# First mixer's heads: a PSUM bank of its own for each of four heads under way, and the grouped heads begun behind a turn's second and third chunk

## The chip, the cores and the metric

The kernel runs on one core of a Trainium2 chip. The metric is the device time of one execution in microseconds (us). Five engines work side by side, each with a queue of its own that it works off in order: PE (TensorE, matrix products into PSUM), DVE (VectorE), ACT (ScalarE), POOL (GpSimd), and SP (SyncE), which here issues the transfers. PSUM has eight banks of 512 fp32 columns by 128 partitions.

## The reference

One inference step of a backbone with two layers, for 128 context tokens and 128 latent tokens, 2048 wide. Layer 0 has the mixer that the change touches: eight heads of latent attention (MLA) and eight of grouped-query attention (GQA) side by side, with one output projection.

```python
def mixer_ab(h, rope, ctx, w_in, g_q, w_q_up, g_kv, w_kv_up, g_qn, g_kn, w_out):
    proj = h @ w_in
    ...
    qb = rmsnorm(proj[..., i2:i3].reshape(b, t, GQA_HEADS, HEAD_DIM), g_qn)
    ...
    qa = (rmsnorm(q_lat, g_q) @ w_q_up).reshape(b, t, MLA_HEADS, MLA_NOPE_DIM + MLA_ROPE_DIM)
    ...
    kv = (ckv_all @ w_kv_up).reshape(b, s, MLA_HEADS, MLA_NOPE_DIM + MLA_V_DIM)
    ...
    out_a = softmax_attention(jnp.concatenate([qa_nope, qa_rope], axis=-1), ka, va, MLA_SCALE)
    out_b = softmax_attention(qb, kb_all, vb_all, HEAD_SCALE)
    out = jnp.concatenate([out_a.reshape(b, t, -1), out_b.reshape(b, t, -1)], axis=-1) @ w_out
    return out, new_ctx
```

`softmax_attention` is a softmax over all keys: a context query sees the 128 context keys, a latent query 128 cached and 128 latent keys. Every sub-layer is modulated by `mod = silu(cond) @ w_ada + b_ada` (shift, scale, gate), and that product is large: the kernel works it off in pieces beside the rest.

## The kernel before

Both groups of tokens go through together as 256 columns, the context first. A weight block comes as fp32 (`raw`), and ACT and DVE split it into `wh` (L248) and `wl` (L249); a product is three matmuls, wh by the high half of the activations, wh by the low half, wl by the high half. `gemm` (L356) does 128 output rows of such a product into one PSUM bank; a call of it is a chunk.

The **heads** of the first mixer are the second half of `mixer_ab`. A loop with h = 0, 2, 4, 6 does two MLA heads and two GQA heads a turn. It calls `gemm` for three chunks of the query weights (WQ: the two heads' `qn`, then their rotated parts `qr`) and for two chunks of the key weights (WK: `kn` of each head, 384 columns); then `values` multiplies out both heads' values for the three blocks of keys (`vm`), and `mla_pair` both heads' scores. ACT copies each chunk out of its bank. The GQA queries lie ready in `qb`; `gqa_query` norms and rotates the next one, `gqa` does one head's scores.

`head_ab` (L895) is a head from its scores on, a generator that goes on by a stage whenever `pump` is called: DVE takes the maxima (L867, L868, `nmx` L872), ACT the exponentials with their sums (L874), DVE scales with the reciprocal sums (`rec` L902, `p` L903, L904), PE transposes three blocks into the one misc bank, ACT copies them out (`pT` L883), PE multiplies with the values into an att bank, and ACT and DVE split that (L248, L249) into `o`, the tile that the trace names `hx`. `o` holds heads 0 to 7 from MLA, 8 to 15 from GQA.

PSUM: three banks go round for the gemms and the value blocks (`acc`), three for scores and head results (`att`), one is `misc`, one `ada`.

Beside the heads two more works run, one step at a `pump`. One is the next modulation's rows on PE (`ada` from `araw`, 32 x 512 each, 16 instructions of the trace to a group). The other, **deep**, does a part of `w_ada` on DVE: `sums` (L525) multiplies a tile of 128 x 1024, `kvb` and `block` in turn, 512 KB each by a transfer on SP, with the conditioning `condb`, and sums it; a tile takes two such instructions, which is called a pair here. The product itself isn't used, and is written to `deep.junk`, `o[:, 6:8]`, where the results of the last two MLA heads come later. Half-way a second `condb` is loaded (L513), and ACT does its Silu (L516, with a load of its function table). Of the 21 pairs that end before the first mixer's output starts anew, 15 use the first half and six the second.

After the heads `out_ab` multiplies by `w_out_ab`. `first_three` does the first three output columns at once, in an order (`PAIR_LATE`) that takes k = 8 to 15 first (GQA), then 0 to 5, and last 6 and 7.

The order of the instructions on each engine isn't written out: the code gives the dependences, and a scheduler at compile time with a cost model of its own orders each queue. Some instructions are pinned to the order of the code (`keep_order`).

Of the kernel before, what the change touches and what calls it, by code (L numbers as in the profile page):

```python
# [16 lines left out]
PSUM = bass.MemoryType.PSUM  # L17

P = 128
# [75 lines left out]
def step_kernel(ctx: ExitStack, tc: tile.TileContext, A: dict):  # L95
# [29 lines left out]
    small = ctx.enter_context(tc.tile_pool(name="small", bufs=4))  # L125
    pacc = ctx.enter_context(tc.tile_pool(name="pacc", bufs=3, space=PSUM))
    pmisc = ctx.enter_context(tc.tile_pool(name="pmisc", bufs=1, space=PSUM))
# [97 lines left out]
    def bank():  # L225
        return T_(pmisc, [P, 512], "misc")

    def att_bank():
        return T_(ppool["att"], [P, 512], "att", bufs=3)

# [101 lines left out]

    def first_three(W, xh, xl, order, mid=None, fixed=False, first=0):


        pin = keep_order if fixed else lambda i: i
        raws = [W.load()[0] for _ in range(3)]
        ps = [T_(pacc, [P, 512], "acc") for _ in range(3)]
        blocks = {(c, h): W.halves(raws[c], 8 * h) for c, h in ((0, first), (1, first), (2, first), (0, 1 - first))}
        count = [0] * 3  # L340
        for n, (c, k) in enumerate(order):
            if mid and n == len(order) // 2:
                mid()
# [12 lines left out]
    def gemm(blocks, xh, xl, n=NT, first=0, between=None, more=None, wider=None):  # L356

        fixed = lambda i: keep_order(i) if between is not None else i  # L360
        ps = T_(pacc, [P, 512], "acc")
        last = len(blocks) - 1
        for i in range(last + 1):
            k = (i + first) % (last + 1)
            wh, wl = blocks[k]
            x0 = more(k) if more and i == 0 else wider(k, 0, n + push.pop(0)) if push else xh(k)
            fixed(pe.matmul(ps[:, :x0.shape[-1]], wh, x0, start=(i == 0), stop=False,
                            skip_group_check=i > 0 and x0.shape[-1] > n))
            if callable(between):
# [463 lines left out]
    def final_rstd(st):  # L833
        cols = [bank(), T_(pacc, [P, 512], "acc")]
# [52 lines left out]

    def scores(q, k):

        s = T_(ppool["att"], [P, 512], "att", bufs=3)  # L890
        for g, ks in KEYS:
            pe.matmul(s[:, ks], q[:, g * T:(g + 1) * T], k[:, ks], start=True, stop=True)
        return s

    def head_ab(pl, s, rs, v, hx, c):  # L895
# [12 lines left out]
        yield  # L908
        o = T_(ppool["att"], [P, 512], "att", bufs=3)
        pe.matmul(o[:, 0:T], v(0), pT[:, 0:T], start=True, stop=True)  # L910
# [5 lines left out]
    def mixer_ab(hx, beside):  # L916
        l = 0
        with tc.tile_pool(name="ab", bufs=1) as ab:
            with tc.tile_pool(name="abp", bufs=1) as pj:
# [187 lines left out]
                def values(c):  # L1107
                    pt = T_(ppool["att"], [P, 512], "att", bufs=3)
                    for g in range(2):
# [106 lines left out]
            with tc.tile_pool(name="abh", bufs=1) as hp:  # L1216
# [24 lines left out]
                def gqa(h):  # L1241
                    k = kg[:, h // 4]
                    return head_ab(hp, scores(qb[:, h], k), rsb[:, h], lambda b: vg[:, b, h // 4], o, 8 + h)

                def values():
# [3 lines left out]
                    for b in range(3):  # L1249
                        ps = T_(pacc, [P, 512], "acc")  # L1250
                        t = slice(b * T, (b + 1) * T)
# [10 lines left out]
                def mla_pair(h, qr, kn, vm):  # L1262
                    s = [T_(ppool["att"], [P, 512], "att", bufs=3) for i in range(2)]
                    for g, ks in KEYS:
# [9 lines left out]
                    for i in range(2):  # L1274
                        start(head_ab(hp, s[i], rsm, lambda b, i=i: vm[:, b, i], o, h + i))

                flush()
                weigh_lambda()
                start(gqa_query(0))
                deep.tiles.append((ab, "kvb"))  # L1280
                deep.junk = o[:, 6:8]
                deep.rate = SIDE["heads"]
                for h in range(0, 8, 2):
                    for i in range(2):
                        ps = gemm(WQ.chunk(), qh, qlo)
                        qn[h + i] = T_(hp, [P, NT], "qn", bufs=4)
                        act.copy(qn[h + i], ps)
                        pump(RATE["heads"])
                    ps = gemm(WQ.chunk(), qh, qlo)
                    ev = T_(tmp, [P, NT], "nt", bufs=4)  # L1290
# [51 lines left out]
    def mixer_c(cp, hx, W, ready, st):  # L1342
# [18 lines left out]
        def turned_product(middle):  # L1361

            ps = [T_(pacc, [P, 512], "acc") for _ in range(2)]
            for k in range(KD):
# [48 lines left out]
        def attend(h, q, k, v):  # L1413
# [3 lines left out]
            for j in range(2):  # L1417
                s = T_(ppool["att"], [P, 512], "att", bufs=3)
                for g, ks in ((0, slice(0, T)), (1, slice(T, 3 * T))):
# [21 lines left out]
            yield  # L1441
            o = T_(ppool["att"], [P, 512], "att", bufs=3)
            pe.matmul(o[:, 0:NT], pT[:, 0:T], v[:, 0], start=True, stop=True)
# [18 lines left out]
            yield  # L1462
            pt = T_(ppool["att"], [P, 512], "att", bufs=3)
            for i in range(2):
# [126 lines left out]
    with banks("pab") as ppool["ada"]:  # L1591
        ppool["att"] = ppool["ada"]
        idle = T_(tmp, [P, 512], "am", bufs=1)
        keep_order(dve.memset(idle, 0.0))
        ps = T_(pacc, [P, 512], "acc")
        for _ in range(WARM):
# [183 lines left out]
```

## Time and profile before

| | us |
|---|---|
| runs | 2303.16, 2305.42, 2304.32 |
| median | 2304.32 |
| profiled execution | 2305.63 |
| its span | 2303.9 |
| heads' first weights to the end of the first three output columns, in the span | 208 to 356 |

The profiled execution has a mean granted clock of 0.995. The page gives busy time by engine, and groups of instructions by line; `acc`, `att`, `misc`, `ada` are PSUM banks, `hx` is `o` there, and `L110` and `L113` are the helpers through which every matmul and transpose goes, so that on PE the tiles tell what an instruction is. A row of the timeline has its start, its duration, engine, line, result and operands, and in brackets the idle time before it with what ended that. A 128-row matmul in fp32 counts twice there.

### The profile page before, as it was taken

To read this page: it belongs to the slowest core of one execution; us is meant where nothing else is said; L and a number is where in the kernel's file an instruction comes from. 1 tells how busy PE (TensorE), PEld (TensorE's weight loads), DVE (VectorE), ACT (ScalarE), POOL (GpSimd) and SP (SyncE) were. 2 spreads that over 40 slices of the span, in tenths; PEclk is the share of its full clock that TensorE was granted. 3 is DMA by queue.
4 is the path that set the end of the run, shared out by engine and by line. 5 is a ranking of instruction groups with operands and counts; after the bars stand their busy time and mean duration, and the time that the engine had idled before them with its cause. 6 is when DMAs were issued, how large, how long until landed. Compare 5 with 4: busy or idle time off the path is not lost.

```text
span 2303.9 us, 47433 instructions
## 1 busy us (share of the span) xinstructions
PE 2271.4 (99%) x19496; PEld 2180.7 (95%) x19496; DVE 1887.7 (82%) x2989; ACT 1197.0 (52%) x1959; POOL 173.5 (8%) x206
## 2 busy tenths in 40 slices
PE   8899999999999999999999999999999999999998
PEld 6788869999999999999999999999999999999998
DVE  4668979989999999999978988898899965666654
ACT  4346555665553355555575454457555434555543
POOL 0001101300000000001130001023000000000011
PEclk9999999999999999999999999999999999999999
DMA  9988878777777777777787888776677755555553
GB/s 380 369 338 302 317 312 342 289 275 264 262 256 290 291 274 259 272 259 257 289 293 292 317 325 313 264 272 227 247 255 262 264 201 188 200 190 195 197 189 127
DMA packets 100121, 617.14 MB, mean 268 GB/s; under 512 B 10752, under 2 KB 18880, under 8 KB 33344
## 3 DMA queue, kind: packets, MB, share of 16 engines
q1 hardware_dynamic: 99904, 614.11, 72.0%
q8 instruction: 153, 2.51, 0.4%
q14 instruction: 64, 0.52, 0.1%
HBM read 609.32 MB, written 4.75 MB: 267 GB/s over the span
## 4 chain that ended last, share of the span: by engine, by line
PE 93%; DVE 3%; DMA 1%; issue 1%; ACT 1%; POOL 1%; SPq 0%; DVEq 0%; ACTq 0%
PE acc L110 87%; PE ada L110 3%; PE att L110 2%; DVE wl L249 1%; DVE hx L525 1%; DMA raw<-w_in_ab 1%; DMA kvb<-w_ada 1%; POOL dev L807 0%; DVE rope L858 0%; PE att L113 0%; PE ada L113 0%; PE misc L110 0%; PE misc L113 0%; ACT wh L248 0%; DVE x L1637 0%
## 5 line engine op out<-in xcount | busy, mean ns | idle before, releaser
L110 PE MATMUL acc<-hx,wh 128*128 128x256 f32 (+1 forms) x7264 | 1254.3, 278 | 4.8 <-ACT wh L248 1.7
L248 ACT CAST wh<-raw 128x1024 fp32r<-128x1024 f32 (+1 forms) x834 | 796.1, 967 | 868.1 <-PE acc L110 741.0
L249 DVE TENSOR_TENSOR wl<-raw,wh 128x1024 fp32r<-128x1024 f32 (+1 forms) x834 | 924.9, 1125 | 247.9 <-ACT wh L248 240.7
L110 PEld LDWEIGHTS acc<-hx,wh 128*128 128x128 f32 x7264 | 1099.5, 188 | 23.4 <-issue 8.1
L110 PE MATMUL acc<-hx,wl 128*128 128x256 f32 (+1 forms) x3632 | 1006.8, 277 | 4.4 <-DVE wl L249 4.3
L110 PEld LDWEIGHTS acc<-hx,wl 128*128 128x128 f32 x3632 | 684.1, 188 | 8.1 <-DVE wl L249 5.6
L110 PE MATMUL acc<-g,wh 128*128 128x256 f32 x2816 | 478.8, 276 | 0.0
L110 PEld LDWEIGHTS acc<-g,wh 128*128 128x128 f32 x2816 | 423.4, 188 | 0.0
L110 PE MATMUL acc<-g,wl 128*128 128x256 f32 x1408 | 388.0, 276 | 0.0
L473 DVE CUSTOM_DVE_ANT_0 junk<-araw,condb 128x2048 f32<-128x2048 f32 x128 | 294.3, 2299 | 0.0
L110 PEld LDWEIGHTS acc<-g,wl 128*128 128x128 f32 x1408 | 264.2, 188 | 0.0
L110 PE MATMUL acc<-hxc,wh 128*128 128x256 f32 (+1 forms) x1056 | 189.1, 281 | 0.0
L211 POOL TENSOR_TENSOR sqacc<-sqacc,sq 128x256 f32<-128x256 f32 x62 | 71.5, 1153 | 1507.7 <-ACT sq L207 1507.5
L110 PEld LDWEIGHTS acc<-hxc,wh 128*128 128x128 f32 x1056 | 161.9, 188 | 1.8 <-issue 1.7
L110 PE MATMUL acc<-hxc,wl 128*128 128x256 f32 (+1 forms) x528 | 146.8, 278 | 0.0
L110 PEld LDWEIGHTS acc<-hxc,wl 128*128 128x128 f32 x528 | 99.5, 188 | 0.2
L110 PE MATMUL acc<-wh,hxc 128*128 128x256 f32 (+1 forms) x512 | 95.0, 283 | 0.8 <-DVE nt L818 0.8
L1530 ACT ACTIVATE cv<-acc,convw 128x256 f32<-128x256 f32 x169 | 94.4, 559 | 0.0
L525 DVE CUSTOM_DVE_ANT_0 hx<-block,condb 128x1024 fp32r<-128x1024 f32 x65 | 79.3, 1219 | 6.2 <-DMA block<-w_ada 6.0
L1536 DVE SCALAR_TENSOR_TENSOR cv<-acc,convw,cv 128x254 f32<-128x254 f32 x169 | 81.0, 479 | 3.2
L843 DVE SCALAR_TENSOR_TENSOR x<-acc,mod,x 128x128 f32<-128x128 f32 x190 | 57.2, 343 | 32.0 <-PE acc L110 32.0
L110 PEld LDWEIGHTS acc<-wh,hxc 128*128 128x128 f32 x512 | 79.4, 188 | 3.7 <-issue 2.5
(265 smaller groups left out, 1784.5 us busy)
## 6 DMA issues: line engine op xcount, KB each, us to landing
raw<-w_up SPq DMA_DIRECT2D x176, 1024.0 KB, 4.8
araw<-w_ada SPq DMA_DIRECT2D x136, 1024.0 KB, 6.0
raw<-w_down SPq DMA_DIRECT2D x88, 1024.0 KB, 4.8
raw<-w_in_c SPq DMA_DIRECT2D x48, 1024.0 KB, 6.4
block<-w_ada SPq DMA_DIRECT2D x41, 512.0 KB, 6.4
raw<-w_in_ab SPq DMA_DIRECT2D x18, 1024.0 KB, 9.2
raw<-w_out_ab SPq DMA_DIRECT2D x16, 1024.0 KB, 7.9
raw<-w_out_c SPq DMA_DIRECT2D x16, 1024.0 KB, 7.1
```

The costliest lines, as they stand in the source:

```text
L110: return self.placed(nc.tensor.matmul(*a, **kw))
L211: eng.tensor_tensor(out=st["acc"], in0=st["acc"], in1=sq, op=ALU.add)
L248: pin(act.copy(out_hi, src))
L249: pin(dve.tensor_tensor(out=out_lo, in0=src, in1=out_hi.bitcast(F32), op=ALU.subtract))
L473: keep_order(dve.tensor_tensor_reduce(out=T_(feat["pool"], [P, D], "junk"), in1=feat["row"][:, c], in0=feat["raw"].rearrange("p g n -> p ( ...
L525: keep_order(dve.tensor_tensor_reduce(out=self.junk, in0=self.raw, in1=self.row[:, c].rearrange("p (g n) -> p g n", g=2), scale=1.0, scala ...
L843: dve.scalar_tensor_tensor(out=x[:, c, s], in0=ps[:, s], scalar=mod[:, l, 3 * which + 2, c, g:g + 1], in1=x[:, c, s], op0=ALU.mult, op1=AL ...
L1530: pin(act.activation(y, ps, AF.Identity, scale=cw[:, 1, m:m + 1], bias=cw[:, 3, m:m + 1]))
L1536: pin(dve.scalar_tensor_tensor(out=y3[:, :, :T - 1], in0=p3[:, :, 1:], scalar=cw[:, 2, m:m + 1], in1=y3[:, :, :T - 1], op0=ALU.mult, op1=A ...
```

## The change

- The three gemm banks get names, acc0 to acc2, one buffer each, and `acc_bank` takes them in turn. During the heads' loop only acc0 and acc1 are in that turn. The three att banks get names in the same way.
- A GQA head's scores go to att0 or att1 by the parity of the head; an MLA pair's to att2 and acc2.
- `head_ab` puts its product with the values in the bank of the scores, in place of a new att bank.
- `begin_gqa` starts the first GQA head of a turn behind the second chunk and the second behind the third; both began ahead of a WK chunk before, behind the third and the fourth.
- `first_three` takes acc0, acc1 and att0.

```diff
@@ -123,7 +123,7 @@
     small = ctx.enter_context(tc.tile_pool(name="small", bufs=4))
-    pacc = ctx.enter_context(tc.tile_pool(name="pacc", bufs=3, space=PSUM))
+    pacc = ctx.enter_context(tc.tile_pool(name="pacc", bufs=1, space=PSUM))
     pmisc = ctx.enter_context(tc.tile_pool(name="pmisc", bufs=1, space=PSUM))
...
@@ -225,8 +225,18 @@
 
-    def att_bank():
-        return T_(ppool["att"], [P, 512], "att", bufs=3)
+    def att_bank(n=None):
+        if n is None:
+            turn["att"], n = (turn["att"] + 1) % 3, turn["att"]
+        return T_(ppool["att"], [P, 512], f"att{n}")
+
+    accs, turn = [0, 1, 2], {"acc": 0, "att": 0}
+
+    def acc_bank(n=None):
+        if n is None:
+            n = accs[turn["acc"] % len(accs)]
+            turn["acc"] += 1
+        return T_(pacc, [P, 512], f"acc{n}")
 
...
@@ -330,12 +340,12 @@
 
-    def first_three(W, xh, xl, order, mid=None, fixed=False, first=0):
+    def first_three(W, xh, xl, order, mid=None, fixed=False, first=0, third=acc_bank):
 
 
         pin = keep_order if fixed else lambda i: i
         raws = [W.load()[0] for _ in range(3)]
-        ps = [T_(pacc, [P, 512], "acc") for _ in range(3)]
+        ps = [acc_bank(), acc_bank(), third()]
         blocks = {(c, h): W.halves(raws[c], 8 * h) for c, h in ((0, first), (1, first), (2, first), (0, 1 - first))}
...
@@ -885,9 +895,8 @@
 
-    def scores(q, k):
-
-        s = T_(ppool["att"], [P, 512], "att", bufs=3)
+    def scores(s, q, k):
+
         for g, ks in KEYS:
...
@@ -906,7 +915,7 @@
         yield
-        o = T_(ppool["att"], [P, 512], "att", bufs=3)
+        o = s
         pe.matmul(o[:, 0:T], v(0), pT[:, 0:T], start=True, stop=True)
...
@@ -1240,14 +1249,14 @@
                     k = kg[:, h // 4]
-                    return head_ab(hp, scores(qb[:, h], k), rsb[:, h], lambda b: vg[:, b, h // 4], o, 8 + h)
+                    return head_ab(hp, scores(att_bank(h % 2), qb[:, h], k), rsb[:, h], lambda b: vg[:, b, h // 4], o, 8 + h)
 
                 def values():
 
                     wh, wl = WK.last_tile()
                     vm = T_(hp, [P, 3, 2, P], "vm", bufs=2)
                     for b in range(3):
-                        ps = T_(pacc, [P, 512], "acc")
+                        ps = acc_bank()
                         t = slice(b * T, (b + 1) * T)
...
@@ -1274,8 +1283,14 @@
 
+                def begin_gqa(h):
+                    if h < 7:
+                        start(gqa_query(h + 1))
+                    start(gqa(h))
+
                 flush()
                 weigh_lambda()
+                accs[:] = [0, 1]
                 start(gqa_query(0))
...
@@ -1286,6 +1301,7 @@
                         pump(RATE["heads"])
+                    begin_gqa(h)
                     ps = gemm(WQ.chunk(), qh, qlo)
...
@@ -1294,16 +1310,15 @@
                     kn = []
+                    begin_gqa(h + 1)
                     for i in range(2):
-                        if h + i < 7:
-                            start(gqa_query(h + i + 1))
-                        start(gqa(h + i))
                         ps = gemm(WK.chunk(), kh, klo, 3 * T)
                         kn.append(T_(hp, [P, 3 * T], "kn", bufs=2))
                         act.copy(kn[i], ps)
                         pump(RATE["heads"])
                     mla_pair(h, qr, kn, values())
                 flush()
+                accs[:] = [0, 1, 2]
 
...
@@ -1317,7 +1332,8 @@
         deep.rate = SIDE["out0"]
-        ready = first_three(W, oh, ol, PAIR_LATE, first=1)
+        turn["acc"] = 0
+        ready = first_three(W, oh, ol, PAIR_LATE, first=1, third=lambda: att_bank(0))
         for c in range(KD):
...
```

The remaining hunks only write `acc_bank()` and `att_bank()` where a bank was asked for by its pool. The number of instructions of every kind is the same. Their order differs in the heads and at the start of the output projection only.

PE, the end of the first turn's values and the MLA scores (`kn` and `qr`). Before, the end of the next turn's third query chunk, behind which the first pair's scores stand:

```order
L110 MATMUL acc_505_2847<-ql_290_1787,wl_498_2810 128x256
L110 MATMUL acc_505_2847<-ql_290_1787,wh_497_2809 128x256 x2
L110 MATMUL acc_505_2847<-ql_290_1787,wl_498_2810 128x256
L110 MATMUL att_474_2720<-pT_471_2700,vg_17_119 128x128 x3
L110 MATMUL ada_476_2729<-araw_446_2591,condw_6_79 32x512 x4
L110 MATMUL ada_476_2729<-araw_448_2595,condw_6_79 32x512 x4
L110 MATMUL att_479_2742<-kn_441_2567,qn_406_2425 128x128
L110 MATMUL att_480_2743<-kn_457_2629,qn_415_2474 128x128
L110 MATMUL att_479_2742<-kr_15_117,qr_425_2512 128x128
L110 MATMUL att_480_2743<-kr_15_117,qr_425_2512 128x128
L110 MATMUL att_479_2742<-kn_441_2567,qn_406_2425 128x256
L110 MATMUL att_480_2743<-kn_457_2629,qn_415_2474 128x256
```

Now, the first turn's first value block (`kv_in`):

```order
L110 MATMUL acc1_469_2673<-wl_450_2583,kv_in_289_1786 128x256
L110 MATMUL acc1_469_2673<-wh_449_2582,kv_in_289_1786 128x256 x2
L110 MATMUL acc1_469_2673<-wl_450_2583,kv_in_289_1786 128x256
L110 MATMUL acc1_469_2673<-wh_449_2582,kv_in_289_1786 128x256
L110 MATMUL att2_477_2740<-kn_452_2599,qn_406_2425 128x128
L110 MATMUL att2_477_2740<-kr_15_117,qr_432_2531 128x128
L110 MATMUL att2_477_2740<-kn_452_2599,qn_406_2425 128x256
L113 MATMUL misc_453_2601<-cst_2_74,p_422_2489 128x128
L110 MATMUL att2_477_2740<-kr_15_117,qr_432_2531 128x256
L113 MATMUL misc_453_2601<-cst_2_74,p_422_2489 128x128 x2
```

The first MLA head's scores moved from behind the next turn's three query chunks, a product with values and an ada group to right behind the first value block of their own turn.

ACT, the first turn's key chunks. `p` with `nmx` is an exponential, `kn` and `vm` are the copies of a gemm's bank. Before:

```order
L1291 COPY nt_424_2510<-acc_423_2491 128x256
L1293 COPY qr_425_2512<-nt_424_2510 128x128
L1303 COPY kn_441_2567<-acc_440_2554 128x384
L1229 ACTIVATE sq_516_2914<-qb_47_242 128x256
L1230 ACTIVATE qb_47_242<-qb_47_242,cst_2_74 128x256
L874 ACTIVATE p_432_2533,sums_431_2532<-att_429_2528,nmx_433_2534,rsb_20_122 128x128
L874 ACTIVATE p_432_2533,sums_431_2532<-att_429_2528,nmx_433_2534,rsb_20_122 128x256
L248 CAST wh_495_2805<-raw_494_2803 128x1024
L1303 COPY kn_457_2629<-acc_456_2616 128x384
L1257 COPY vm_466_2661<-acc_467_2662 128x256
```

Now:

```order
L1307 COPY nt_431_2529<-acc0_430_2510 128x256
L1238 ACTIVATE sq_503_2845<-qb_47_242 128x256
L1309 COPY qr_432_2531<-nt_431_2529 128x128
L1239 ACTIVATE qb_47_242<-qb_47_242,cst_2_74 128x256
L884 ACTIVATE p_422_2489,sums_421_2488<-att0_419_2484,nmx_423_2490,rsb_20_122 128x128
L884 ACTIVATE p_422_2489,sums_421_2488<-att0_419_2484,nmx_423_2490,rsb_20_122 128x256
L1317 COPY kn_452_2599<-acc1_451_2586 128x384
L258 CAST wh_493_2803<-raw_492_2801 128x1024
L1317 COPY kn_463_2648<-acc0_462_2635 128x384
L1266 COPY vm_468_2672<-acc1_469_2673 128x256
```

The copy of the first `kn` stood ahead of the first exponential, and now stands behind it.

DVE, the end of the deep pairs ahead of the last MLA heads' split (`hx` from `att` or `acc`; `ISA` is an instruction of a pair). Before:

```order
L902 RECIPROCAL rec_745_3890<-sums_742_3882 128x2
L249 TENSOR_TENSOR wl_769_4049<-raw_755_3927,wh_768_4048 128x512
L525 ISA hx_394_2383,mod_4_77<-kvb_733_3854,condb_605_3291 128x1024
L525 ISA mod_4_77 128x1
L903 TENSOR_SCALAR p_743_3883<-p_743_3883,rec_745_3890 128x128
L904 TENSOR_SCALAR p_743_3883<-p_743_3883,rec_745_3890 128x256
L249 TENSOR_TENSOR wl_769_4049<-raw_755_3927,wh_768_4048 128x512
L249 TENSOR_TENSOR wl_771_4073<-raw_756_3929,wh_770_4072 128x512 x2
L249 TENSOR_TENSOR wl_782_4166<-raw_780_4163,wh_781_4165 128x1024
L723 TENSOR_TENSOR u_753_3924<-mod_4_77,u_753_3924 128x4x2
L249 TENSOR_TENSOR hx_394_2383<-att_750_3906,hx_394_2383 128x256
L249 TENSOR_TENSOR hx_394_2383<-att_751_3912,hx_394_2383 128x256
```

Now:

```order
L535 ISA hx_394_2383,mod_4_77<-block_710_3766,condb_608_3315 128x1024
L535 ISA mod_4_77 128x1
L535 ISA hx_394_2383,mod_4_77<-block_710_3766,condb_608_3315 128x1024
L535 ISA mod_4_77 128x1
L535 ISA hx_394_2383,mod_4_77<-kvb_719_3840,condb_608_3315 128x1024
L535 ISA mod_4_77 128x1
L535 ISA hx_394_2383,mod_4_77<-kvb_719_3840,condb_608_3315 128x1024
L535 ISA mod_4_77 128x1
L259 TENSOR_TENSOR hx_394_2383<-att2_720_3844,hx_394_2383 128x256
L259 TENSOR_TENSOR hx_394_2383<-acc2_721_3845,hx_394_2383 128x256
```

The two splits stood behind weight splits that followed the last pair, and now stand right behind the last pair, of which there are two in a row that wait for their own transfers.

More of the change, by code (lines that the diff above doesn't have):

```diff
@@ L833, in final_rstd @@
     def final_rstd(st):
-        cols = [bank(), T_(pacc, [P, 512], "acc")]
+        cols = [bank(), acc_bank()]
         for src, start in ((st["acc"], True), (st["last"], False)):
@@ L1107, in values @@
                 def values(c):
-                    pt = T_(ppool["att"], [P, 512], "att", bufs=3)
+                    pt = att_bank()
                     for g in range(2):
@@ L1249, in values @@
                     for b in range(3):
-                        ps = T_(pacc, [P, 512], "acc")
+                        ps = acc_bank()
                         t = slice(b * T, (b + 1) * T)
@@ L1262, in mla_pair @@
                 def mla_pair(h, qr, kn, vm):
-                    s = [T_(ppool["att"], [P, 512], "att", bufs=3) for i in range(2)]
+                    s = [att_bank(2), acc_bank(2)]
                     for g, ks in KEYS:
@@ L1361, in turned_product @@
         def turned_product(middle):
-            ps = [T_(pacc, [P, 512], "acc") for _ in range(2)]
+            ps = [acc_bank() for _ in range(2)]
             for k in range(KD):
@@ L1417, in attend @@
             for j in range(2):
-                s = T_(ppool["att"], [P, 512], "att", bufs=3)
+                s = att_bank()
                 for g, ks in ((0, slice(0, T)), (1, slice(T, 3 * T))):
@@ L1441, in attend @@
             yield
-            o = T_(ppool["att"], [P, 512], "att", bufs=3)
+            o = att_bank()
             pe.matmul(o[:, 0:NT], pT[:, 0:T], v[:, 0], start=True, stop=True)
@@ L1462, in attend @@
             yield
-            pt = T_(ppool["att"], [P, 512], "att", bufs=3)
+            pt = att_bank()
             for i in range(2):
@@ L1594, in step_kernel @@
         keep_order(dve.memset(idle, 0.0))
-        ps = T_(pacc, [P, 512], "acc")
+        ps = acc_bank()
         for _ in range(WARM):
```

## The prediction

> **What bounds the kernel now.** The page first: it says which engine sets the span.
>
> ```profile
> PE 2271.4 (99%) x19496; PEld 2180.7 (95%) x19496; DVE 1887.7 (82%) x2989; ACT 1197.0 (52%) x1959; POOL 173.5 (8%) x206
> ```
>
> PE is busy 99% of the span, so a change that leaves its instructions as they are can gain only what PE waits for, and what the clock loses behind a wait. The second view is therefore PE's waits between 208 and 356 us, from the first chunk of the heads to the end of the first three output columns; outside it the order of the instructions is the same in both kernels. Columns: engine, what waited, what it waited for, us in total, times, longest.
>
> ```profile
> PE misc L113 <- DVE p L903: 2.9, 2, 2.7
> PE acc L110 <- ACT vm L1257: 1.7, 2, 1.4
> PE att L110 <- DVE hx L249: 1.2, 1, 1.2
> PE misc L113 <- ACT pT L883: 0.6, 1, 0.6
> PE att L110 <- ACT pT L883: 0.2, 1, 0.2
> ```
>
> They sum to 6.6 us in 148. The change speaks of the second and third (a bank that is not yet read out); the longest waits for DVE to scale a head's probabilities. The third view, windows around that longest one (length, PE busy, PEld, DVE, ACT, POOL, granted clock, DMA share, GB/s), shows what it costs beyond itself.
>
> ```profile
> 325.00:329.00 4.00, 4.00 (x32) 2.91 (x24) 3.63 (x9) 0.74 (x2) 0.00 (x0) 1.00 0.73 260
> 329.00:332.00 3.00, 0.29 (x2) 0.30 (x3) 2.26 (x10) 1.92 (x7) 0.93 (x2) 0.77 0.98 411
> 332.00:336.00 4.00, 4.00 (x19) 0.77 (x18) 3.01 (x6) 0.76 (x3) 0.00 (x0) 0.50 0.71 245
> 336.00:339.00 3.00, 3.00 (x23) 2.88 (x20) 2.56 (x8) 1.44 (x3) 0.00 (x0) 0.76 0.91 363
> ```
>
> After the wait PE runs at half clock: of the last 0.3 us of the second row, the 4.00 of the third and 1.4 of the fourth (0.76 is about 1.44 us at half in 3), 5.7 us of work, half of which, 2.9 us, is lost. [...] The stage thus holds 6.6 + 2.9 = 9.5 us: the most that the change can bring.
>
> The fourth view is DVE from the heads' first weights to the end of the fifteenth pair of its deep reductions (L525, 1024 columns against a transfer of 512 KB), and what it waits for there.
>
> ```profile
> 210.30:301.40 91.10, 82.34 (x208) 1.00 0.84 322
> ```
>
> ```profile
> DVE hx L525 <- DMA block<-w_ada: 5.4, 4, 2.5
> DVE hx L525 <- DMA kvb<-w_ada: 2.2, 2, 1.3
> ```
>
> DVE is busy 82.3 of 91.1 us, and 7.6 of its 8.8 idle us wait for those transfers. It is the second bound, and it works in order.
>
> **The change part by part.** *Banks.* The count of every kind of instruction stays. The gemms of the stage rotate over two banks in place of three, so a gemm now writes the bank of the chunk two back. The first place where this shows is the first block of values in the first turn. Before, it starts at 223.91, and no bank is late:
>
> ```profile
> 222.46 1.07 PE L110 MATMUL ada<-araw,condw 128*32 128x512 f32 x8
> 223.46 0.44 PE L110 MATMUL acc<-kv_in,wh 128*128 128x384 f32 x1
> 223.91 0.28 PE L110 MATMUL acc<-wh,kv_in 128*128 128x256 f32 x1
> ```
>
> On ACT, and on DVE the maxima that release it, the same moments were these:
>
> ```profile
> 223.18 0.46 ACT L874 ACTIVATE p<-att,nmx,rsb 128x128 f32<-128x128 f32 x1 [1.73 <-DVE nmx L872]
> 223.63 0.56 ACT L874 ACTIVATE p<-att,nmx,rsb 128x256 f32<-128x256 f32 x1
> 224.17 1.04 ACT L248 CAST wh<-raw 128x1024 fp32r<-128x1024 f32 x1
> 225.11 0.48 ACT L1303 COPY kn<-acc 128x384 f32<-128x384 f32 x1
> ```
>
> ```profile
> 222.99 0.15 DVE L872 SCALAR_TENSOR_TENSOR nmx<-mx,rsb 128x2 f32<-128x2 f32 x1
> ```
>
> In the new order one half of an ada group (223.46 - 222.46 = 1.00 us) no longer stands ahead, so PE arrives at 222.9. The block now needs the bank whose read-out (kn) stands on ACT behind the first grouped head's two exponentials (223.18 to 224.17, the read of the sum included). Their maxima come some 1 us earlier than 222.99, since the scores do: 222.15 + 1.0 + 0.48 = 223.6. That is a new PE wait of 0.7 us, bounded by 0 (maxima 1 us earlier still) and 2 (as late as before: 224.17 + 0.48 - 222.9 = 1.75). Behind it on PE stand the block itself and the MLA scores, which need its bank order; later turns have more distance between chunk and copy, so I put all four turns at W = 1.5 us, with 0 and 8 as ends.
>
> *Heads' own banks, and where they begin.* The MLA scores no longer wait for an att bank that another head's result holds (the 1.2 us row), and stand a turn's third earlier. More of PE's work thereby stands ahead of the first output column, worked out from issue intervals in these rows:
>
> ```profile
> 237.48 0.83 PE L110 MATMUL att<-pT,vg 128*128 128x128 f32 x6
> 238.24 1.92 PE L110 MATMUL ada<-araw,condw 128*32 128x512 f32 x16
> 240.09 0.71 PE L110 MATMUL att<-kn,qn 128*128 128x128 f32 x4
> 240.73 0.49 PE L110 MATMUL att<-kr,qr 64*128 64x128 f32 x4
> 241.15 1.13 PE L110 MATMUL att<-kn,qn 128*128 128x256 f32 x4
> 242.21 0.70 PE L110 MATMUL att<-kr,qr 64*128 64x256 f32 x4
> 242.85 0.50 PE L110 MATMUL acc<-ql,wh 128*128 128x256 f32 x2
> ```
>
> ```profile
> 308.03 0.50 PE L110 MATMUL misc<-cst,sq 128*128 128x1 f32 x4
> 308.40 0.91 PE L110 MATMUL att<-pT,vg 128*128 128x128 f32 x6
> 309.07 0.48 PE L110 MATMUL acc<-hx,wh 128*128 128x256 f32 x2
> ```
>
> Two MLA heads' scores take 242.85 - 240.09 = 2.76 us, one grouped head's (the kn half of those) 0.85, probabilities by values 0.7, an ada group 1.85. The new order has ahead of that column 4 MLA scores (5.5), 2 grouped (1.7), 4 products with values (2.8), 5 sets of transposes (1.9, at the 0.37 of the misc row), 2 ada groups (3.7), and two smaller things (0.4 each: 308.40 - 308.03): 16.4 us more. It started at 309.07 with 3.0 us of waits before it (1.2, 1.7 and 0.2 of the list), so it now starts at 309.07 - 3.0 + 16.4 = 322.4, plus W. What follows it is as much shorter, and by PE alone the first three columns would end 9.5 us sooner than before, at 355.7 - 9.5 = 346.2.
>
> *What is late next.* These columns end on the last two MLA heads (k = 6 and 7), and their split into hi and lo stands behind the last deep pair, on ACT too: the reductions' unused output goes to the place of these two heads, so ACT may not write it before. The deep chain is thus on the path. It is released by the second half's Silu, which ACT does behind the split of a grouped head:
>
> ```profile
> 309.54 0.38 ACT L248 CAST hx<-att 128x256 fp32r<-128x256 f32 x1
> 311.55 1.28 ACT L516 ACT_TABLE_LOAD   x1
> 312.85 1.91 ACT L516 ACTIVATE condb<-condb 128x2048 f32<-128x2048 f32 x1
> 314.66 0.35 ACT L248 CAST hx<-att 128x256 fp32r<-128x256 f32 x1
> ```
>
> What a step of the chain lasts (mean ns behind the busy time), and how long a transfer takes to land (median us):
>
> ```profile
> L525 DVE CUSTOM_DVE_ANT_0 hx<-kvb,condb 128x1024 fp32r<-128x1024 f32 x20 | 24.4, 1219 | 4.2 <-DMA kvb<-w_ada 4.1
> L249 DVE TENSOR_TENSOR wl<-raw,wh 128x512 fp32r<-128x512 f32 x17 | 11.2, 686 | 0.4 <-ACT wh L248 0.4
> ```
>
> ```profile
> block<-w_ada SPq DMA_DIRECT2D x11, 512.0 KB, 6.4
> kvb<-w_ada SPq DMA_DIRECT2D x10, 512.0 KB, 7.1
> ```
>
> Before, Silu starts at 312.85, while PE has work of the columns. Now that grouped head's product stands 4.1 us of PE work ahead of the columns: 322.4 - 4.1 = 318.3; split 0.38, table load 1.30, Silu 1.81: S = 321.8 + W. Six pairs follow, each 2 x 1.2 us. Pair 16: S + 2.4. Its block is then refilled (6.4): S + 8.9, and pair 18 with a head's scaling (0.6) ends at S + 11.9; four half-tiles of wl (4 x 0.6) and some narrow steps (0.5) go before pair 19, which with a whole wl (1.2) between ends at S + 18.6. On SP the transfer of pair 21 waits for that, behind two weight transfers. It lands 6.4 to 7.1 us later (I take 6.4, as no other transfer is ahead then), so pair 21 ends at S + 27.4; the two splits and the last six rows take 1.9. The columns end at 321.8 + 29.3 + W = 351.1 + W, against 355.7:
>
> ```profile
> 355.73 1.92 PE L110 MATMUL ada<-araw,condw 128*32 128x512 f32 x16
> ```
>
> That is 4.6 us sooner, less W. PE stands idle for about 5 us before its last 18 rows, longer than the 2.7 of the third view, so it pays half clock again: 0 to 2.9 us; the last rows and the ada group are short work, so I take 2.0.
>
> DVE has to do 35 more rows (five heads' maxima, scalings and splits) ahead of the fifteenth pair, some 7 us in a stretch that had 8.8 idle. Since the Silu waits for PE at 318 and the pair ended at 301, this cover holds with 10 us to spare.
>
> **Sum.** Gain 4.6, less 1.5, less 2.0: 1.1 us. Of the profiled execution's 2305.63 us (its span 2303.9 and 1.7 around it) 2304.5 remain; that execution lies 1.31 above the median of the runs, 2304.32, so the forecast is 2303.2. About 0.2%, 4.6 us, is what a measurement of this kernel can tell from no change.
>
> **The rivals.** *Faster.* The transfers land quicker than 6.4, because the second Silu's successors no longer wait on SP behind an output weight that came late before. Two landings lie in the chain; at 5 us each, with W at 0.7 and the clock kept, the gain is 4.6 + 2.8 - 0.7 = 6.7: 2297.6. For it: the transfer for pair 17 is issued right behind the second conditioning half. Against: the medians 6.4 and 7.1 are of this very stage, at a DMA share of 0.84. The bound is 9.5, or 2294.8.
>
> *Slower.* Two banks are too few: each turn, PE waits for a copy that ACT does behind an exponential, and that behind DVE's maxima. At 2 us in each of four turns W is 8: 351.1 + 8 + 2.0 - 355.7 = 5.4 us slower, 2309.7. It decides from W = 2.6 (no gain left) and tells from W = 7.2. For it: DVE's 90% and the vm row, 1.4 us with three banks. Against: ACT is busy half the time, and a chunk takes some 2 us of PE, so that a copy has that long. [...]
>
> *No effect.* The heads start no sooner, since their scores wait for qn, kn and the rotations anyway, and the tail ends where it did: 2304.3.
>
> **Chances.** The forecast's case, with the one of no effect, has 0.50; faster by over 0.2% 0.28; slower by over 0.2% 0.22, since in-order queues with so many moved rows hold waits that this sum didn't see. The range goes from 2296.0 (between the faster rival and the bound) to 2309.5 (just under W = 8), which leaves out about 2 in 10.
>
> **What would show it.** Right: PE's list of waits has lost the row on hx and the 2.7 on p; a new one on kn or vm, 0.7 in the first turn and some 1.5 in all; Silu near 322 to 324; a PE wait of some 5 us on hx shortly before the end of the columns at 351 to 353, with the clock at half behind it. Wrong: no such wait at the end and the columns at 346 (faster); waits on ACT copies of 2 us in every turn (slower); or Silu before 318, in which case the chain has another release.

## The result

The changed kernel takes 2308.95 us (median of 18 runs, 2306.59 to 2314.85), the kernel before 2305.30 on the same chips (18 runs): a ratio of 1.0016, 95% interval 1.0010 to 1.0023. It is 3.65 us slower. The time lies in the range given, but on the other side of the forecast of 1.1 us faster.

The profiled execution took 2308.26 us (span 2306.5), 2.6 more than that of before. Where these lie can be read from PE's waits in the same stage, 208 to 360 us:

```profile
PE acc L110 <- ACT hx L258: 7.1, 1, 7.1
```

All five rows of before are gone, and one of 7.1 us has come, the split of the last two MLA heads. Windows around it (length, PE, PEld, DVE, ACT, POOL, clock, DMA share, GB/s):

```profile
349.00:352.00 3.00, 0.00 (x0) 0.00 (x0) 0.71 (x1) 0.00 (x0) 0.00 (x0) 0.75 0.30 123
352.00:355.00 3.00, 0.75 (x3) 0.75 (x4) 2.53 (x7) 0.74 (x3) 0.00 (x0) 0.50 0.04 10
355.00:358.00 3.00, 3.00 (x21) 2.86 (x23) 0.47 (x3) 0.57 (x1) 0.00 (x0) 0.61 0.47 171
```

PE stands still, and most of its last 18 rows run at half clock (granted 0.50 from 352 to 355, 0.61 from 355 to 358). In the chain of waits (start, us, what) one sees what held it:

```profile
332.35 8.85 DMA kvb<-w_ada
...
344.76 6.39 DMA kvb<-w_ada
...
351.29 1.23 DVE hx L535
...
352.56 1.22 DVE hx L535
...
353.82 0.38 ACT hx L258
...
354.25 0.80 PE acc L110 x2
```

That is the chain of the forecast: two refills of a deep tile, the last pair, the split, the last rows. It begins later than forecast, as ACT and PE show:

```profile
321.77 0.37 ACT L258 CAST hx<-att 128x256 fp32r<-128x256 f32 x1 [1.09 <-PE att L110]
322.16 1.28 ACT L526 ACT_TABLE_LOAD   x1
323.45 1.91 ACT L526 ACTIVATE condb<-condb 128x2048 f32<-128x2048 f32 x1
```

The transfer that the Silu needs, by SP's timeline and by the list of transfers (median us to landing):

```profile
312.16 0.61 SPq L523 DMA_DIRECT2D condb<-condb  x1
```

```profile
condb<-condb SPq DMA_DIRECT2D x1, 1024.0 KB, 7.3
```

On PE, up to the columns' start and at their end:

```profile
318.00 0.70 PE L110 MATMUL att<-kr,qr 64*128 64x256 f32 x2
318.62 1.06 PE L110 MATMUL ada<-araw,condw 128*32 128x512 f32 x8
...
326.09 0.70 PE L110 MATMUL acc<-kr,qr 64*128 64x256 f32 x2
326.72 0.50 PE L110 MATMUL att<-hx,wh 128*128 128x256 f32 x2
...
357.95 1.93 PE L110 MATMUL ada<-araw,condw 128*32 128x512 f32 x16
```

The columns begin at 326.7, not 322.4, without any wait ahead of them, and end at 357.95 against 355.73 before. The 2.2 us stay to the end of the span (2.6). In the rows of kr and qr is a reason that the sum didn't have. The trace counts each of these fp32 products twice, so that x2 is one head's: with 64 contraction rows and 256 columns it takes 318.62 - 318.00 = 0.62 us. Both heads' together (x4) took 0.64 in the kernel before (242.21 to 242.85).

### The profile page after: what moved, and what is told of

It reads as the page before. It is cut to its first block, busy times and chain, and to the rows that moved or that the text cites. A ratio compares the mean times of both kernels' runs of the same rounds, so it can differ in the third digit from the quotient of the medians.

```text
span 2306.5 us, 47432 instructions
## 1 busy us (share of the span) xinstructions
PE 2274.7 (99%) x19496; PEld 2182.4 (95%) x19496; DVE 1888.4 (82%) x2989; ACT 1195.9 (52%) x1959; POOL 176.6 (8%) x206
## 4 chain that ended last, share of the span: by engine, by line
PE 95%; DVE 1%; DMA 1%; POOL 1%; ACT 0%; issue 0%; SPq 0%; DVEq 0%; ACTq 0%
PE acc L110 89%; PE ada L110 3%; PE att L110 2%; DMA raw<-w_in_ab 1%; DMA kvb<-w_ada 1%; DVE wl L259 1%; PE misc L110 0%; PE ada L113 0%; POOL dev L817 0%; PE att L113 0%; PE misc L113 0%; DVE x L1653 0%; POOL hxc L821 0%; DVE hx L535 0%; SPq L973 0%
## 5 line engine op out<-in xcount | busy, mean ns | idle before, releaser
L211 POOL TENSOR_TENSOR sqacc<-sqacc,sq 128x256 f32<-128x256 f32 x62 | 76.5, 1234 | 1520.1 <-ACT sq L207 1519.9
```

The lines of the kernel that those rows point to most:

```text
L211: eng.tensor_tensor(out=st["acc"], in0=st["acc"], in1=sq, op=ALU.add)
```

## The experiments

Two theories were set up. **The tail**: the end hangs on the deep chain, because its unused output (`deep.junk`, the junk below) stands where the last heads' result goes. **The pairs**: with a bank of its own the first MLA head's scores go ahead as soon as its keys are copied, and the two heads' 64-row products, which used to stand next to each other, cost twice as much (0.62 us for one head's at 256 columns, where both heads' together took 0.64). The rivals: DVE has too much to do, whatever holds the split (the backlog); and it is the earlier beginnings of the grouped heads, not the banks.

Two things limit what a run can show. The kernels ran on several chips, so where kernels of different chips are set side by side below, it is by their distances from the kernel before on the same chip. And the scheduler orders the queues anew for each edit. By the traces up to 515 us, PE, DVE and ACT keep the order of the kernel that a run starts from only where the junk is moved in the kernel before, and nearly so where it is moved beside the pinned pairs; with the thin sums PE keeps it. Everywhere else a difference is that of the edit together with the order that came of it.

| kernel | median, us | before, same chip | ratio (95%) |
|---|---|---|---|
| change, junk moved | 2312.59 | 2305.76 | 1.0027 (1.0016 to 1.0038) |
| change, pairs pinned | 2306.57 | 2305.76 | 1.0005 (0.9996 to 1.0014) |
| change, both | 2306.57 | 2305.76 | 1.0004 (0.9995 to 1.0013) |
| before, junk moved | 2305.99 | 2305.76 | 1.0000 (0.9991 to 1.0008) |
| banks alone | 2304.62 | 2305.04 | 0.9996 (0.9987 to 1.0005) |
| beginnings alone | 2307.78 | 2305.04 | 1.0012 (1.0003 to 1.0021) |
| before, pairs parted | 2308.78 | 2305.04 | 1.0016 (1.0007 to 1.0025) |
| change, junk moved, thin sums | 2301.13 | 2305.04 | 0.9981 (0.9972 to 0.9990) |
| change, one conditioning | 2300.80 | 2305.60 | 0.9977 (0.9968 to 0.9986) |
| before, one conditioning | 2308.39 | 2305.60 | 1.0013 (1.0004 to 1.0022) |
| banks, junk moved | 2300.16 | 2305.60 | 0.9979 (0.9971 to 0.9988) |
| banks, pairs pinned | 2311.79 | 2305.60 | 1.0029 (1.0018 to 1.0040) |

From the timelines of their profiled executions, in us from the span's start:

| kernel | pair 15 ends | Silu starts | last pair ends | columns' results read |
|---|---|---|---|---|
| before | 301.4 | 312.9 | 347.9 | 355.4 |
| banks alone | 307.8 | 319.9 | 350.2 | 354.2 |
| beginnings alone | 307.6 | 319.8 | 354.0 | 356.6 |
| change | 312.1 | 323.5 | 353.8 | 357.6 |
| change, pairs pinned | 304.4 | 316.2 | 352.4 | 355.9 |
| change, junk moved | 313.3 | 324.7 | 358.4 | 350.0 |
| banks, junk moved | 307.0 | 319.0 | 348.6 | 346.4 |

**The junk moved**, in the changed kernel. GQA queries 0 to 3 have been used when the last turn begins.

```diff
                 for h in range(0, 8, 2):
+                    if h == 6:
+                        deep.junk = qb[:, 0:4].rearrange("p (a b) n -> p a (b n)", a=2)
```

> The changed kernel, with the unused output of the deep reductions' last pairs written to GQA queries that are used up (qb of heads 0 to 3), in place of the last MLA heads' place in o. Theory (the tail): the PE wait of 7.1 us on hx, and the half clock behind it, come from the last MLA heads' split standing behind the last deep pair. Then the wait falls below 1 us, the first three columns end at 348 to 350 in place of 358.0, and the time is 2300 to 2303, 6 to 9 us below the changed kernel. Rival (DVE's backlog): the five heads' more work on DVE made the last heads late anyway; the wait on hx stays within 2 us of 7.1, the columns end at 356 to 358, and the time is 2307 to 2309.

Measured: 2312.6 us, outside both. The wait went and the columns were read at 350.0, 7.6 us sooner, as the tail's theory has it. But further on, from 360 to 460 us, PE waits where it had not waited:

```profile
PE acc L110 <- ACT u L732: 7.0, 1, 7.0
PE acc L110 <- DVE u L733: 2.4, 1, 2.4
```

```profile
430.00:440.00 10.00, 7.45 (x63) 7.10 (x61) 10.00 (x23) 4.23 (x10) 2.70 (x4) 1.00 0.69 252
440.00:450.00 10.00, 3.24 (x13) 2.95 (x14) 7.97 (x23) 8.51 (x27) 9.45 (x15) 0.60 0.04 14
```

These are the last modulation's shifts, which come out of the deep reductions; DVE is full in the first window. So the wait on the split was due to the junk's place. The time behind it is put down to DVE, which the thin sums below test: its last pair ended 4.6 us later than in the change (358.4), and PE got to the end of the projection before it.

**The pairs pinned**, in the changed kernel, and then both edits.

```diff
-                            pe.matmul(s[i][:, ks], qn[h + i][:, g * T:(g + 1) * T], kn[i][:, ks],
-                                      start=True, stop=False)
+                            keep_order(pe.matmul(s[i][:, ks], qn[h + i][:, g * T:(g + 1) * T], kn[i][:, ks],
+                                                 start=True, stop=False))
...
-                            if i:
-                                keep_order(m)
+                            keep_order(m)
```

> The changed kernel, with all eight matmuls of an MLA pair's scores pinned in the order of the code, so that the two 64-row products of the two heads stand next to each other again. Theory (the pairs): two 64-row products next to each other run side by side on PE; apart, they cost double (0.31 in place of 0.16 us for 256 columns), some 4 us over eight heads, which came ahead of the Silu. Then the kr rows take 0.16 and 0.11 us again, Silu starts 3 us sooner, at 320 to 321, and the time is 2304.5 to 2306.5. Rival (the transfer): Silu is held by the second conditioning half, which landed at 319.5, and by the wait for the deep pairs' transfers; the time stays at 2308 to 2309.5.

> Both edits, the junk moved and the pairs pinned. If both theories hold, their gains add for the most part: the columns end at 345 to 347, and the time is 2296 to 2300, below the kernel before. If only the tail counts: 2300 to 2303, as with the junk moved alone. If DVE's backlog counts: 2305 to 2309.

Measured: 2306.6 us for either, 0.8 above the kernel before, where the change is 3.65 above; that is just over the range of the pairs' theory. With the pairs pinned alone, the Silu came at 316.2, sooner than forecast. But PE now waits for both heads' keys and banks; the longest three of seven rows, 7.7 us in all:

```profile
PE misc L113 <- DVE p L912: 2.6, 2, 2.2
PE att L110 <- DVE hx L259: 1.7, 1, 1.7
PE att L110 <- DVE qb L871: 1.1, 1, 1.1
```

With these waits the kernel is where it was before, and there the junk's place changes nothing. That both edits together land in the range set for DVE's backlog is chance: PE has no wait between 360 and 460 us there.

**The junk moved in the kernel before**, by the same edit.

> The kernel before, with the junk moved in the same way. Theory (the tail): in the kernel before, the last splits at 351.3 and 353.6 waited for PE's products, 3 us and more behind the last deep pair (347.8), so nothing changes: 2304 to 2306. Rival (the deep chain held it there too): 3 us and more faster, 2300 to 2302.

Measured: 2305.99 us, no change, with the queues in the same order. Before, the deep pairs ended ahead of the split that PE's products released.

**The halves of the change.** For the banks alone, the grouped heads begin as before; for the beginnings alone, `begin_gqa` is put into the kernel before at the two places.

```diff
-                    begin_gqa(h)
                     ps = gemm(WQ.chunk(), qh, qlo)
...
-                    begin_gqa(h + 1)
                     for i in range(2):
+                        begin_gqa(h + i)
                         ps = gemm(WK.chunk(), kh, klo, 3 * T)
```

> The banks of the change alone; the grouped heads begin where they did before, ahead of each key chunk. Theory (the banks part the pairs): with a bank of its own, the first MLA head's scores are issued as soon as its key chunk is copied, and the two heads' 64-row products no longer stand together; the kr rows keep most of their 0.2 and 0.3 us, and the time is 2307 to 2310, as with the whole change. Rival (the beginnings): it is the earlier grouped heads that crowd DVE; without them the time is 2304 to 2306.

> The beginnings of the change alone, behind the second and third chunk, with the banks of before (three gemm banks and three for heads in turn). Theory (the banks part the pairs): the pairs stay together at 0.11 and 0.16 us, PE's waits stay about the 6.6 us of before, and the time is 2304 to 2307. Rival (the beginnings crowd DVE): 2308 to 2310, with the last deep pair at 351 or later.

Measured: 2304.6 and 2307.8 us. The banks alone don't cost anything; the beginnings alone cost 2.7 us, just under the rival's range. That speaks for the rival: with the beginnings alone all four pairs stand together, and the kr rows take 4.2 us in the stage, against 5.3 before and 7.7 in the change, so that the 2.7 us aren't the pairs'. By the second table each half delays the fifteenth pair by about 6 us. In return the banks rid PE of all its waits of before; what it has is one on the last split (and 0.5 us on a transfer):

```profile
PE acc L110 <- ACT hx L258: 5.7, 1, 5.7
```

The beginnings alone give nothing in return; PE waits 8.2 us in the stage, more than the 6.6 of before, and the last pair ends at 354.0, just ahead of the split (the longest three of five rows):

```profile
PE misc L113 <- ACT pT L883: 3.4, 2, 2.8
PE acc L110 <- ACT hx L248: 2.1, 2, 1.7
PE misc L113 <- DVE p L903: 1.6, 2, 1.1
```

**The pairs parted**, in the kernel before: the loop over the heads goes outside, and all is pinned.

```diff
-                    for g, ks in KEYS:
-                        for i in range(2):
...
+                    for i in range(2):
+                        for g, ks in KEYS:
```

> The kernel before, with the scores of an MLA pair issued head by head, pinned in that order, so that the 64-row products never stand next to each other; nothing else changes. Theory (the pairs): three of the four pairs stood together before, so six heads pay 0.10 and 0.16 us twice each, 3.1 us of PE work ahead of the output projection, and the time is 2308 to 2309.5. Rival (the work is hidden or the doubled rows are only shown so by the trace): 2305 to 2306.5.

Measured: 2308.8 us, 3.7 more, as the pairs' theory has it. The timeline of PE at the first pair shows the price by itself:

```profile
239.88 0.49 PE L110 MATMUL att<-kn,qn 128*128 128x128 f32 x2
240.30 0.48 PE L110 MATMUL att<-kr,qr 64*128 64x128 f32 x2
240.72 0.70 PE L110 MATMUL att<-kn,qn 128*128 128x256 f32 x2
241.35 0.70 PE L110 MATMUL att<-kr,qr 64*128 64x256 f32 x2
...
244.06 0.50 PE L110 MATMUL acc<-ql,wh 128*128 128x256 f32 x2
```

Two heads take 244.06 - 239.88 = 4.18 us, against 2.76 before: 1.42 for this pair, about 1.0 of it in the kr rows and 0.4 in the kn rows. The profiled execution, 2306.49 us, is one of the shortest of this kernel's eleven, and its columns end where those of before end. Counted from one row's start to the next, its kr and kn rows take 3.9 us more in the stage. Two things make up for that: its 2.7 us wait on p did not bring half clock (the granted clock is 1.00 from 300 to 360), where the kernel before lost 2.9 us by it, and its waits are 1.4 us shorter. So the rows show the price of the pairs and the runs a loss of that size. But the edit also pins all eight products, which has a price of its own (below), and the runs don't tell the two apart.

**DVE relieved at the end.** The changed kernel with the junk moved, and shorter sums in the output projection:

```diff
+            w = 256 if self.thin else 512
             keep_order(dve.tensor_tensor_reduce(
-                out=self.junk, in0=self.raw, in1=self.row[:, c].rearrange("p (g n) -> p g n", g=2),
+                out=self.junk[:, :, :w], in0=self.raw[:, :, :w],
+                in1=self.row[:, c].rearrange("p (g n) -> p g n", g=2)[:, :, :w],
...
         deep.rate = SIDE["out0"]
+        deep.thin = True
```

> The changed kernel with the junk moved, and with the deep reductions that are begun in the output projection done over half of their columns (a part of the modulation is left out), which takes some 0.6 us off each of about 26 DVE instructions. Theory (DVE's backlog): with the junk moved, PE reached the output projection's end sooner than DVE, and waited 9.4 us there for the last modulation; with DVE some 15 us ahead, that wait and the half clock behind it go, and the time is 2297 to 2301. Rival (only an unlucky order of the queues): the wait on u stays above 5 us, and the time is 2308 to 2313.

Measured: 2301.1 us. That is 3.9 below the kernel before, where the same kernel with whole sums is 6.8 above: 10.7 us less. Of the 9.4 us on u, 1.0 is left:

```profile
PE acc L110 <- ACT u L735: 0.6, 1, 0.6
PE acc L110 <- DVE u L736: 0.4, 1, 0.4
```

So DVE's lateness at the end is what took the moved junk's gain. PE's order is the same as with whole sums; DVE's differs in many places from 371 us on, and how much of its lateness is work and how much order is not shown.

**One conditioning**, in the changed kernel and in the kernel before:

```diff
-                    self.steps += [lambda: self.cond(1)] + [lambda: None] * 3 + [self.silu, lambda: None]
+                    self.steps += ([lambda: None] * 6 if len(units) == 4 else
+                                   [lambda: self.cond(1)] + [lambda: None] * 3 + [self.silu, lambda: None])
```

Of the two stages that use these steps, this one alone has four units.

> The changed kernel without the second conditioning half in this stage: its transfer and its Silu are left out, and the last six pairs are multiplied by the first half's values (so that part of the modulation is computed from other data). Theory (the chain from pair 15 on): the transfer starts only when the fifteenth pair frees the buffer (312.2), Silu ends 13 us later, and the last six pairs and the split hang on that. Without it the pairs follow at once and end some 10 us sooner, near 342, the wait of 7.1 us on hx goes, and the time is 2299 to 2302. Rival (DVE is full anyway): the wait comes back at the end of the projection, on u, as with the junk moved, and the time is 2306 to 2312.

> The kernel before, without the second conditioning half in the same way. Theory (the chain): the kernel before had its fifteenth pair at 301.4 and its last at 347.8, ahead of the last splits, which PE's products released; it gains only what DVE's earlier work takes off the waits on p (2.9 us and the half clock behind): 2300 to 2304. If the chain bounded it as much as the changed kernel: 2296 to 2299.

Measured: 2300.8 and 2308.4 us. In the changed kernel the wait of 7.1 went and no other came in the stage; the last pair ended at 345.4, 8.4 us sooner, and the last split stands right behind it:

```profile
345.83 0.42 DVE L259 TENSOR_TENSOR hx<-att,hx 128x256 fp32r<-128x256 f32 x1 [0.44 <-ACT hx L258]
346.17 0.41 DVE L259 TENSOR_TENSOR hx<-acc,hx 128x256 fp32r<-128x256 f32 x1
348.08 1.13 DVE L854 SCALAR_TENSOR_TENSOR x<-acc,mod,x 128x128 f32<-128x128 f32 x4 [1.43 <-PE acc L110]
```

The kernel before got slower by 2.8 us where 1.6 to 5.6 us of gain were expected: its longest wait, on a head's scaling, went from 2.7 to 5.6 us.

```profile
PE misc L113 <- DVE p L904: 5.6, 1, 5.6
```

DVE's timeline shows why. In the kernel before, the scaling stands ahead of a deep pair that waits for its transfer:

```profile
331.28 0.29 DVE L903 TENSOR_SCALAR p<-p,rec 128x128 f32<-128x128 f32 x1
...
333.67 1.23 DVE L525 CUSTOM_DVE_ANT_0 hx<-kvb,condb 128x1024 fp32r<-128x1024 f32 x1 [0.61 <-DMA kvb<-w_ada]
```

Without the second conditioning it stands behind that pair:

```profile
331.37 1.23 DVE L526 CUSTOM_DVE_ANT_0 hx<-kvb,condb 128x1024 fp32r<-128x1024 f32 x1 [1.31 <-DMA kvb<-w_ada]
...
333.80 0.28 DVE L904 TENSOR_SCALAR p<-p,rec 128x128 f32<-128x128 f32 x1
```

The wait is 2.9 us longer by that, about the 2.8 lost. Why the scheduler chose this order with the six steps gone is not shown. So the second conditioning is worth some 8 us in the changed kernel, with the order that came of leaving it out, and no gain came of it in the kernel before.

**Without the harmful half.** The banks alone, with the junk moved, and with the pairs pinned:

> The banks of the change alone, with the junk moved. There the last split waited 5.7 us for the last deep pair. If the tail's wait is all: it goes, and the time is 2297 to 2300, below the kernel before. If DVE's backlog takes its place at the end of the projection, as with the whole change: 2304 to 2310.

> The banks of the change alone, with the pairs pinned. The 64-row products lose the 1.9 us that they took more than when next to each other, but the pin makes PE wait for both heads' keys, as in the whole change with the pin (7.7 us of waits in the stage). I expect these to cancel: 2303 to 2306. If the pairs' work alone counts: 2301 to 2303.

Measured: 2300.2 and 2311.8 us. The first, at the edge of the tail's range, is below both kernels, 5.4 us below the kernel before (0.9979, interval 0.9971 to 0.9988). PE waits 1.2 us in the whole stage, 1.0 of it at once, the columns are read from 346.4 on, and DVE's last pair, at 348.6, comes 10 us sooner than with the beginnings (358.4):

```profile
PE acc L110 <- DVE wl L259: 1.0, 1, 1.0
```

Part of the 9.0 us is given back at the end of the projection, where PE waits once and the clock sinks for a while:

```profile
PE att L110 <- ACT sq L207: 1.1, 1, 1.1
```

```profile
430.00:440.00 10.00, 8.86 (x63) 8.78 (x62) 7.57 (x24) 4.87 (x15) 2.22 (x5) 0.83 0.43 157
```

The pinned one lies above both ranges: behind the pin PE waits 5.2 us for a copy of values, and the last splits come at 357 and 358.5. What waits there is the first product of the output's columns (at 323.34), for the gemm bank that this copy empties: the wait that the slower rival named, in another place.

```profile
PE acc L110 <- ACT vm L1266: 5.2, 1, 5.2
```

By the distances from the kernel before, pinning for the pairs is thus worth 2.8 us with the beginnings and costs 6.6 without them. Its effect depends on what else the queue is made to wait for.

## Why the prediction was wrong

- **Banks, W = 1.5 us: too high.** No wait came on a gemm bank. In the first turn the maxima were 1.2 us sooner than put, and the copy of kn ended at 222.5, when PE arrived.
- **PE's work ahead of the columns: the first step that failed.** It was summed to 16.4 us more than before and the start put at 322.4; with no wait at all it came at 326.7. Counted from one row's start to the next, the work had grown by 20.7 us. The MLA scores (kn and kr) grew from 5.7 to 14.4, by 8.7 where 5.5 was put, which is 3.2 of the 4.3 us missing. Each MLA head was priced at 1.38 us, half of the 2.76 of a pair whose products stand together, while the quoted order shows the first head alone. All four pairs now stand ahead of the columns: three of them are parted, and the third pair is parted in its 128-column half. The other 1.1 us are the balance of smaller terms, mainly these: ada groups took 4.4 us for 3.7 and the gemms, which more other rows now interrupt, 1.9 more, where the grouped heads' scores took 0.4 for 1.7. In the traces the 64-row products of two heads next to each other cost as much as those of one head apart (0.64 us for four, 0.62 for two, at 256 columns).
- **DVE's cover: the second.** The 35 more rows were put at 7 us, to be taken from 8.8 idle us, and the cover at 10. The fifteenth pair ended 10.7 us later (312.1 for 301.4). The sum forgot that the second conditioning half is only fetched when that pair has freed its buffer; it was issued at 312.16, lasted 7.3 us and landed at 319.5, so that of the 10 us of cover some 7 were the transfer's. The Silu started at 323.45, where 320.0 plus W was put. In this execution ACT waited last for PE's product (1.09 us, at 321.77), so that PE's lateness is the nearer cause; the transfer had landed 2.3 us earlier.
- **The chain from the Silu to the last pair: right in kind, 28.4 us for 27.4.** It ran over another refill than in the sum: that of pair 19, issued at 332.35, which took 8.85 us, where the sum had DVE's own work between pairs 18 and 19.
- **The last rows: right.** 357.95 - 353.8 = 4.1 us, 1.9 of work and 2.0 for the clock in the sum.
- **Sum.** 354.6 was put for the columns' end, 357.95 came: 2.1 from the Silu (3.6 late, less the 1.5 of W that didn't come), 1.0 from the chain, 0.2 from the last rows. The rivals named neither: slower was to come from gemm banks, and those never held PE. Of the signs, the Silu's time (323.45), the wait on hx and the half clock behind it came; the columns' end did not.
- **What the whole change hid.** Its halves work against each other. The banks took away 6.6 us of waits and paid with DVE's lateness; the beginnings alone paid as much of it for nothing, and the prediction had not priced the two apart at all.

Open: why the scheduler sets the scaling behind the pair in the kernel before without the second conditioning; how much of the parted kernel's 3.7 us is the pin's; and how much of DVE's lateness behind the moved junk is work and how much order.

## What to carry over

When waits go from an engine that is never idle otherwise, look for a side chain that ends at the same point: here a reduction's unused output, whose place cost nothing before, took what the banks had gained, and one line that put it elsewhere, together with the banks alone, gave 5.4 us. Read from the order which instructions stand next to each other before pricing them from a trace in which they stood otherwise. And a change in two parts is priced part by part: one of these two only moved work on an engine that was already busy 82.3 of 91.1 us.

## What the runs showed of the hardware

- In the kernel before, two heads' matmuls with 64 contraction rows each, on different halves of the rows and into different banks, ran side by side where they stood next to each other. In the trace, which counts each such fp32 product twice, instructions of the two then start 0.01 us apart (242.21 and 242.22), and the four of both heads take 0.64 us for 256 columns and 0.42 for 128. Where another product stood between, in the changed kernel and with the pairs parted, one head's two took 0.62 and 0.42 by themselves.
- A wait of 2.7 us was followed by half clock in the kernel before (0.50 from 330.6 to 337.4, 6.8 us) and was not in the profiled execution with the pairs parted (1.00 from 300 to 360). With the banks alone and the junk moved, 1.1 us of waiting came with a lower clock: 0.83 over the 10 us from 430 to 440, by which the author puts 3.4 us of them at half clock, an estimate. What decides whether a wait is followed by half clock, and for how long, is not shown.
